# Linear attention with its output gate projected at another place, copies of turned tiles on ScalarE, and rows of scales made in two steps

## The chip, the cores and the metric

One core of a Trainium2 chip runs the whole program. The metric is the device time of one execution in microseconds (us), lower is better. Engines are named as in the profile: PE is TensorE, DVE is VectorE, ACT is ScalarE, POOL is GpSimd, SP issues most DMAs. PEld is PE's weight load, which runs beside its matmuls.

## What is computed

Four transformer-like layers over 256 tokens of 1024 numbers, all in float32: a forgetting attention and an MLP, a latent attention (MLA) and an MLP, then a gated linear attention (GLA) with a convolutional MLP and a short-convolution mixer with another one. The change touches GLA most:

```python
def gla_mixer(h, w_in, w_gate_up, b_gate, head_norm_g, w_out):
    proj = h @ w_in
    q, k, v, g, a_low = ...                 # widths 512, 512, 1024, 1024, 16
    log_a = jax.nn.log_sigmoid(a_low @ w_gate_up + b_gate) / 16.0
    bcum = jnp.cumsum(lc, axis=3)           # inside chunks of 64 tokens
    q_in = qc * jnp.exp(bcum)
    k_in = kc * jnp.exp(-bcum)
    scores = jnp.where(mask, jnp.einsum('bhncd,bhnsd->bhncs', q_in, k_in), 0.0)
    o_intra = jnp.einsum('bhncs,bhnse->bhnce', scores, vc)
    k_dec = kc * jnp.exp(b_last[..., None, :] - bcum)
    chunk_kv = jnp.einsum('bhncd,bhnce->bhnde', k_dec, vc)
    ...                                     # a scan over 4 chunks adds o_inter
    o = o * lax.rsqrt(jnp.mean(o * o, axis=-1, keepdims=True) + RMS_EPS)
    o = o * head_norm_g * jax.nn.silu(g)
    return o @ w_out
```

## The kernel before

**Matmuls in three parts.** Each weight tile is loaded raw by SP's queue, rounded to a high part on ACT (`wh`, L294) and subtracted to a low part on DVE (`wl`, L312). Each activation is split the same way (`hh` L509 or L1373, `hl` L512 or L1374). Each product is three matmuls: high by high, high by low, low by high (L339). A unit is two blocks of 128 weight rows; there are five buffers for split units, and `unit` casts four units ahead, at the call that takes a unit.

**Projections.** `proj` multiplies 8 blocks of activations by a weight block of 512 columns for two groups of 128 tokens (t = 0 and 1): after each t of each block, three matmuls, it calls `tick`, so a projection has 16 ticks. Its results stand in two of the three PSUM banks of the tag `up`; after the last block of each t an `evac` function reads them. `proj_T` makes the turned product (features in partitions) with 96 matmuls of 256 columns, 16 ticks as well; `proj_wide` one of 528 columns. `accum` is the output projection into four banks of the tag `acc`; of its inputs `y` it first takes blocks 0 to 3 and then 4 to 7.

**Deferred steps.** `after(n, f)` puts a step n ticks later into the order of the program. `force` runs the deferred steps at once where something that is asked for isn't emitted yet (`Act.get` does this for an operand). The tile framework then fixes each engine's order at compile time, by its own estimate of when each instruction is ready, with the order of the program as priority; on the chip each engine runs that order and waits where an operand is late.

**GLA before** (`gla`, L1151): `proj_wide` gives the first half of v and the 16 gate columns; `proj` of the second half of v follows, and beside it `gates` and `gates2` (two rounds of a log-sigmoid chain of DVE and ACT steps, a scaling by 1/16 at L1205, a scan at L1208, four exponentials). Then `proj_T` of k into acc banks and of q into up banks (`ev_k`, `ev_q` multiply by a row of scales, L416 and L419), then `proj` of the first half g0 of the output gate with the side program `core` beside it, and then `proj` of its second half g1. `core` makes one step per tick from tick 4 of the projection it stands beside: scores, states, at tick 12 the outputs `o` of heads 0 and 1 with their square sums, at tick 13 those of heads 2 and 3. `ev_g` applies Silu on ACT (L1248) and, some ticks later, the head gain on DVE (L1251); `fin` multiplies the outputs by their root scale and the gate (L1342); `prep` turns the result on PE into the one bank of tag `tp` (L523), and `split` makes `hh` on ACT and `hl` on DVE from that bank. Then `accum` runs.

**Rows of scales.** `make_row` (L137) copies two columns of scales wide on DVE (L144), turns them on PE with `transpose4` in the same step, and copies the row out on ACT (L148). There are seven in the program.

**Attention.** `pT` (L721) turns probabilities into two banks; DVE empties one (L725), ACT the other (L726). There are 12 calls. MLA also turns its rotated keys (L1035) and queries (L1072) and empties those banks on DVE.

Of the kernel before, what the change touches and what calls it, by code (L numbers as in the profile page):

```python
# [11 lines left out]
F32 = mybir.dt.float32  # L12
# [6 lines left out]
P = 128  # L19
# [100 lines left out]
class Cols:  # L120


    def __init__(self, kb, tile):
        self.kb, self.tile, self.ok, self.rows = kb, tile, set(), {}
# [12 lines left out]
    def make_row(self, c, tp=None):  # L137

        if c in self.rows:
            return  # L140
        kb, nc = self.kb, self.kb.nc
        self.wait(c, c + 2)
        wide = kb.tmp_tile()
        nc.vector.tensor_copy(wide[:, :S].rearrange("p (t n) -> p t n", t=2),  # L144
                              self.tile[:, c:c + 2].unsqueeze(2).to_broadcast([P, 2, P]))
        tp = kb.transpose4(wide, 2, tp if tp is None else lambda: tp)
        row = kb.small.tile([P, S], F32, tag="rowb", name=kb.name("rowb"), bufs=2)
        nc.scalar.copy(row, tp[:, :S])  # L148
        self.rows[c] = row

    def row(self, c, n=2):

        while c not in self.rows:
            if c in self.ok and c + 1 in self.ok:
                self.make_row(c)
            else:
                self.kb.force()
        return self.rows[c].unsqueeze(1).to_broadcast([P, n, S])


class Builder:
# [559 lines left out]
    def pT(self, p):  # L721
        pt = self.att.tile([P, 768], F32, tag="pT", name=self.name("pT"), bufs=2)
        tps = self.halves([p[:, i * P:(i + 1) * P] for i in range(6)], (self.tp_tile, self.attention_tile))
        out = pt.rearrange("p (b j c) -> p b j c", j=2, c=64)
        self.nc.vector.tensor_copy(out[:, :, 0], tps[0])  # L725
        self.nc.scalar.copy(out[:, :, 1], tps[1])  # L726
        return pt
# [265 lines left out]
    def mla(self, h, rs, hook):  # L993
# [21 lines left out]
        def ev_kv(t, ps):  # L1015
# [8 lines left out]
            def rot():  # L1024

                kr = self.tmp_tile(S)
                k3 = kr.rearrange("p (t c) -> p t c", t=2)
                self.rope(k3[:, :, 0:64], kc.rearrange("p (t c) -> p t c", t=2), None, 2)
                nc.vector.tensor_copy(k3[:, :, 64:128], k3[:, :, 0:64])

                def tr():
                    tp = turned()[:, 0:S]
                    for i in range(2):
                        nc.tensor.transpose(tp[:, i * P:(i + 1) * P], kr[:, i * P:(i + 1) * P], self.ident)
                    nc.vector.tensor_copy(krT, tp)  # L1035
                    self.marks.update((("kr", 0), ("kr", 1)))
                self.after(DLY[9], tr)
# [26 lines left out]
        def ev_rope(t, ps):  # L1064
# [5 lines left out]
            def tr():  # L1070
                tp = self.transpose4(o)
                nc.vector.tensor_copy(qr.rearrange("p (k s) -> p k s", k=4)[:, :, t * P:(t + 1) * P],  # L1072
                                      tp.rearrange("p (k s) -> p k s", k=4))
                self.marks.add(("qr", t))
# [68 lines left out]
    def plan_gla(self):  # L1143
        w = self.a["gla_w_in_2"][0]
        self.add_proj(self.a["gla_w_va"], 8, 0, WIDE)
        for c in (1536, 512, 0, 2048, 2560):
            self.add_proj(w, 8, c, 512)
        self.plan_rows(self.a["gla_w_out_2"][0], 0, 4)
        self.plan_rows(self.a["gla_w_out_2"][0], 4, 4)

    def gla(self, h, rs, hook):  # L1151
# [38 lines left out]
        def gates2():  # L1190
# [6 lines left out]
            for j in range(2):  # L1197
                zs = self.tmp_tile()
                for i in range(2):
                    nc.vector.tensor_scalar(out=zs[:, i * S:(i + 1) * S], in0=z[2 * j + i][:, 0:S],  # L1200
                                            scalar1=bg[:, 2 * j + i:2 * j + i + 1], scalar2=None, op0=ALU.add)
# [3 lines left out]
                nc.vector.tensor_scalar(out=o, in0=o, scalar1=1.0 / 16.0, scalar2=None, op0=ALU.mult)  # L1205
# [4 lines left out]
            nc.scalar.activation(out=E, in_=B, func=AF.Exp)  # L1210
            nc.scalar.activation(out=Ei, in_=B, func=AF.Exp, scale=-1.0)
            b4 = B.rearrange("p (n c) -> p n c", c=64)
            bl = b4[:, :, 63:64]
            nc.scalar.activation(out=dec, in_=bl.rearrange("p n c -> p (n c)"), func=AF.Exp)
            nc.vector.tensor_tensor(out=Ed.rearrange("p (n c) -> p n c", c=64), in0=bl.to_broadcast([P, 16, 64]),
                                    in1=b4, op=ALU.subtract)
            nc.scalar.activation(out=Ed, in_=Ed, func=AF.Exp)

        self.after(DLY[16], gates)
        self.proj(h, 8, 512, ev_v(1))  # L1220
# [22 lines left out]
        y = Act(self)  # L1243

        def ev_g(i):
            def f(t, ps):
                gs = self.tmp_tile()
                nc.scalar.activation(out=self.like(gs, ps), in_=ps, func=AF.Silu, scale=rs[:, t:t + 1])  # L1248

                def gain():  # L1250
                    nc.vector.tensor_tensor(out=gs, in0=gs, in1=hg[:, i * 512:(i + 1) * 512], op=ALU.mult)  # L1251
                    self.after(DLY[20], lambda: fin(t, i, gs))

                self.after(DLY[19], gain)
            return f

        oo = {}
# [3 lines left out]
        def core():  # L1261
# [56 lines left out]
            for j in range(2):  # L1318
# [15 lines left out]
                self.rsqrt(hr[:, 4 * j:4 * j + 4], hs[:, 4 * j:4 * j + 4])  # L1334
                yield 1

        def fin(t, j, gs):
            o = oo.pop((t, j))
# [12 lines left out]
        self.proj(h, 8, 512, ev_g(0))  # L1351
        while self.side is not None:
            self.step()
        self.proj(h, 8, 512, ev_g(1))
# [398 lines left out]
```

## Time and profile before

| what | us |
|---|---|
| median of 3 runs (lowest to highest) | 1104.21 (1104.09 to 1104.54) |
| the profiled execution | 1104.49 |
| its span, first to last instruction | 1102.7 |
| mean granted TensorE clock | 0.997 |
| PE busy in the span | 1087.3 |
| DVE busy | 801.4 |
| ACT busy | 609.2 |

1.8 us of the profiled execution lie outside its span. Matmuls are pipelined, and the profile models their ends: a row's duration is longer than the distance to the next start, so PE's lost time is read from start to start, and a wait row shows a little less than was lost.

### The profile page before, as it was taken

To read this page: it belongs to the slowest core of one execution; us is meant where nothing else is said; L and a number is where in the kernel's file an instruction comes from. 1 tells how busy PE (TensorE), PEld (TensorE's weight loads), DVE (VectorE), ACT (ScalarE), POOL (GpSimd) and SP (SyncE) were. 2 spreads that over 40 slices of the span, in tenths; PEclk is the share of its full clock that TensorE was granted. 3 is DMA by queue.
4 is the path that set the end of the run, shared out by engine and by line. 5 is a ranking of instruction groups with operands and counts; after the bars stand their busy time and mean duration, and the time that the engine had idled before them with its cause. 6 is when DMAs were issued, how large, how long until landed. Compare 5 with 4: busy or idle time off the path is not lost.

```text
span 1102.7 us, 19201 instructions
## 1 busy us (share of the span) xinstructions
PE 1087.3 (99%) x7769; PEld 1003.4 (91%) x7769; DVE 801.4 (73%) x1200; ACT 609.2 (55%) x927; POOL 30.4 (3%) x55
## 2 busy tenths in 40 slices
PE   9999999999999999999999999999999999999997
PEld 7987999999988999999897899999999999999996
DVE  6687756556687766555788578787787768987786
ACT  6466655445665555545664556555555446565563
POOL 1000000000000000000010000000000000000001
PEclk9999999999999999999999999999999999999998
DMA  9844466655563566665555354566665664657551
GB/s 335 298 165 145 162 195 206 210 193 173 142 207 128 172 192 204 206 200 192 194 180 183 108 178 155 179 197 217 201 220 193 197 204 153 189 194 224 188 166 74
DMA packets 137801, 207.30 MB, mean 188 GB/s; under 512 B 10528, under 2 KB 65008, under 8 KB 137712
## 3 DMA queue, kind: packets, MB, share of 16 engines
q1 hardware_dynamic: 136576, 203.89, 56.8%
q10 hardware_dynamic: 1136, 2.17, 0.5%
q8 instruction: 61, 1.00, 0.4%
q14 instruction: 28, 0.23, 0.1%
HBM read 204.97 MB, written 1.07 MB: 187 GB/s over the span
## 4 chain that ended last, share of the span: by engine, by line
PE 87%; DVE 7%; ACT 2%; DMA 1%; issue 1%; SPq 0%; ACTq 0%; DVEq 0%
PE up L339 52%; PE acc L339 33%; DVE wl L312 2%; DMA raw<-fox_w_in 1%; ACT wh L294 1%; PE acc L523 1%; PE tp L523 1%; ACT p L697 1%; DVE p L716 1%; DVE x L602 0%; DVE p L707 0%; PE tp L533 0%; DVE tmp L1365 0%; DVE pT L725 0%; DVE kT L1232 0%
## 5 line engine op out<-in xcount | busy, mean ns | idle before, releaser
L312 DVE TENSOR_TENSOR wl<-raw,wh 128x1024 fp32r<-128x1024 f32 (+2 forms) x373 | 452.3, 1219 | 223.4 <-ACT wh L294 222.4
L294 ACT CAST wh<-raw 128x1024 fp32r<-128x1024 f32 (+2 forms) x373 | 388.8, 1043 | 381.7 <-PE up L339 253.1
L339 PE MATMUL up<-hh,wh 128*128 128x256 f32 x1564 | 431.7, 276 | 0.0
L339 PE MATMUL up<-hh,wl 128*128 128x256 f32 x1564 | 430.1, 275 | 0.0
L339 PE MATMUL up<-hl,wh 128*128 128x256 f32 x1564 | 429.4, 275 | 0.0
L339 PEld LDWEIGHTS up<-hh,wh 128*128 128x128 f32 x1564 | 300.1, 192 | 2.9 <-issue 1.5
L339 PEld LDWEIGHTS up<-hh,wl 128*128 128x128 f32 x1564 | 300.1, 192 | 0.9
L339 PEld LDWEIGHTS up<-hl,wh 128*128 128x128 f32 x1564 | 299.8, 192 | 0.3 <-DVE hl L512 0.2
L339 PE MATMUL acc<-wh,hh 128*128 128x512 f32 (+1 forms) x606 | 227.4, 375 | 0.2 <-DVE mx L716 0.2
L339 PE MATMUL acc<-wh,hl 128*128 128x512 f32 (+1 forms) x606 | 225.1, 371 | 0.1
L339 PE MATMUL acc<-wl,hh 128*128 128x512 f32 (+1 forms) x606 | 224.8, 371 | 0.0
L339 PEld LDWEIGHTS acc<-wh,hl 128*128 128x128 f32 x606 | 114.5, 189 | 15.4 <-DVE hl L1374 0.5
L339 PEld LDWEIGHTS acc<-wh,hh 128*128 128x128 f32 x606 | 114.6, 189 | 15.0 <-DVE mx L716 0.6
L339 PEld LDWEIGHTS acc<-wl,hh 128*128 128x128 f32 x606 | 114.7, 189 | 13.4
L1365 DVE SCALAR_TENSOR_TENSOR tmp<-tmp,vecs,tmp 128x255 f32<-128x255 f32 x192 | 78.0, 479 | 15.2 <-ACT tmp L1363 15.2
L339 PE MATMUL up<-wh,hh 128*128 128x512 f32 (+4 forms) x142 | 52.2, 370 | 1.8 <-DVE tmp L419 1.8
L339 PE MATMUL up<-wl,hh 128*128 128x512 f32 (+4 forms) x142 | 49.9, 352 | 0.2 <-DVE wl L312 0.2
L339 PE MATMUL up<-wh,hl 128*128 128x512 f32 (+4 forms) x142 | 49.8, 353 | 0.1
L1363 ACT ACTIVATE tmp<-tmp,vecs 128x256 f32<-128x256 f32 x96 | 40.9, 496 | 0.0
L1373 ACT CAST hh<-tmp 128x512 fp32r<-128x512 f32 x58 | 34.1, 619 | 8.3 <-DVE tmp L1418 8.3
L1374 DVE TENSOR_TENSOR hl<-tmp,hh 128x512 fp32r<-128x512 f32 x58 | 38.3, 685 | 0.0
L339 PEld LDWEIGHTS up<-wh,hh 128*128 128x128 f32 x142 | 26.8, 189 | 8.1 <-issue 5.5
(205 smaller groups left out, 769.8 us busy)
## 6 DMA issues: line engine op xcount, KB each, us to landing
raw<-ffn_w_up SPq DMA_DIRECT2D x176, 256.0 KB, 4.2
raw<-ffn_w_up SPq DMA_DIRECT2D x32, 1024.0 KB, 5.3
raw<-ffn_w_down SPq DMA_DIRECT2D x32, 1024.0 KB, 5.0
raw<-ffn_w_down SPq DMA_DIRECT2D x44, 512.0 KB, 6.6
raw<-sc_w_in SPq DMA_DIRECT2D x12, 1024.0 KB, 5.3
raw<-fox_w_in SPq DMA_DIRECT2D x10, 1024.0 KB, 9.7
raw<-gla_w_in SPq DMA_DIRECT2D x10, 1024.0 KB, 5.0
raw<-fox_w_out SPq DMA_DIRECT2D x4, 1024.0 KB, 5.2
```

Source lines behind the costliest of these rows:

```text
L294: self.last_hi = nc.scalar.copy(hi[:, :kn, :w], self.raws[r][:, k:k + kn])
L312: self.last_wl = nc.vector.tensor_tensor(out=u.lo[:, :kn, :w], in0=self.raws[r][:, k:k + kn], in1=u.hi[:, :kn, :w].bitcast(F32), op=ALU.su ...
L339: self.nc.tensor.matmul(out, lhsT, rhs, start=start, stop=stop, skip_group_check=True)
L523: self.nc.tensor.transpose(tp[:, i * P:(i + 1) * P], src[:, i * P:(i + 1) * P], self.ident)
L697: self.nc.scalar.activation(out=p[:, o:o + n], in_=p[:, o:o + n], func=AF.Exp, scale=scale, bias=nm[:, j:j + 1], accum_out=sm[:, j:j + 1])
L716: self.nc.vector.tensor_tensor_reduce(out=p[:, o:o + n], in0=lgs[h][:, w], in1=bias(h)[:, w], scale=1.0, scalar=NEG, op0=ALU.add, op1=ALU. ...
L1363: nc.scalar.activation(out=out, in_=z, func=AF.Copy, scale=w[:, 2:3])
L1365: nc.vector.scalar_tensor_tensor(out=out[:, d:], in0=z[:, :S - d], scalar=w[:, 2 - d:3 - d], in1=out[:, d:], op0=ALU.mult, op1=ALU.add)
L1373: nc.scalar.copy(hi, src)
L1374: nc.vector.tensor_tensor(out=lo, in0=src, in1=hi.bitcast(F32), op=ALU.subtract)
```

## The change

1. In GLA the weight block of g0 (column 2048) is planned and projected ahead of the second half of v; g1 is now the projection beside `core`, and nothing stands between it and the output projection. The gate g0 is kept in the two buffers of tag `pT` until `fin`; `fin(t, 0)` is deferred by 4 + t ticks from the step that makes the outputs of heads 0 and 1, and no longer by the gate. 
2. In `gates2` the bias is added on ACT (Identity), and the scaling by 1/16 is folded into the exponentials.
3. `make_row` defers its transpose and copy by 3 ticks behind the wide copy.
4. `pT` empties both banks on ACT; MLA's turned keys and queries are emptied on ACT.

```diff
-    def make_row(self, c, tp=None):
-
-        if c in self.rows:
+    def make_row(self, c, tp=None, gap=3):
+
+        if c in self.asked:
             return
+        self.asked.add(c)
...
-        tp = kb.transpose4(wide, 2, tp if tp is None else lambda: tp)
-        row = kb.small.tile([P, S], F32, tag="rowb", name=kb.name("rowb"), bufs=2)
-        nc.scalar.copy(row, tp[:, :S])
-        self.rows[c] = row
+
+        def turn():
+            bank = kb.transpose4(wide, 2, None if tp is None else lambda: tp)
+            row = kb.small.tile([P, S], F32, tag="rowb", name=kb.name("rowb"), bufs=2)
+            nc.scalar.copy(row, bank[:, :S])
+            self.rows[c] = row
+
+        kb.after(gap, turn)
...
-        self.nc.vector.tensor_copy(out[:, :, 0], tps[0])
-        self.nc.scalar.copy(out[:, :, 1], tps[1])
+        for j, tp in enumerate(tps):
+            self.nc.scalar.copy(out[:, :, j], tp)
...
-                    nc.vector.tensor_copy(krT, tp)
+                    nc.scalar.copy(krT, tp)
...
-                nc.vector.tensor_copy(qr.rearrange("p (k s) -> p k s", k=4)[:, :, t * P:(t + 1) * P],
-                                      tp.rearrange("p (k s) -> p k s", k=4))
+                nc.scalar.copy(qr.rearrange("p (k s) -> p k s", k=4)[:, :, t * P:(t + 1) * P],
+                               tp.rearrange("p (k s) -> p k s", k=4))
...
-        for c in (1536, 512, 0, 2048, 2560):
+        for c in (2048, 1536, 512, 0, 2560):
...
-                    nc.vector.tensor_scalar(out=zs[:, i * S:(i + 1) * S], in0=z[2 * j + i][:, 0:S],
-                                            scalar1=bg[:, 2 * j + i:2 * j + i + 1], scalar2=None, op0=ALU.add)
+                    nc.scalar.activation(out=zs[:, i * S:(i + 1) * S], in_=z[2 * j + i][:, 0:S], func=AF.Identity,
+                                         bias=bg[:, 2 * j + i:2 * j + i + 1])
...
-                nc.vector.tensor_scalar(out=o, in0=o, scalar1=1.0 / 16.0, scalar2=None, op0=ALU.mult)
...
-            nc.scalar.activation(out=E, in_=B, func=AF.Exp)
-            nc.scalar.activation(out=Ei, in_=B, func=AF.Exp, scale=-1.0)
+            nc.scalar.activation(out=E, in_=B, func=AF.Exp, scale=1.0 / 16.0)
+            nc.scalar.activation(out=Ei, in_=B, func=AF.Exp, scale=-1.0 / 16.0)
...
+        def ev_g(i):
+            def f(t, ps):
+
+                gs = self.tmp_tile() if i else self.att.tile([P, 768], F32, tag="pT", name=self.name("gs"), bufs=2)[:, :512]
+                nc.scalar.activation(out=self.like(gs, ps), in_=ps, func=AF.Silu, scale=rs[:, t:t + 1])
+
+                def gain():
+                    nc.vector.tensor_tensor(out=gs, in0=gs, in1=hg[:, i * 512:(i + 1) * 512], op=ALU.mult)
+                    gates_of[t, i] = gs
+                    if i:
+                        self.after(DLY[20], lambda: fin(t, i))
+
+                self.after(DLY[19], gain)
+            return f
+
+        self.proj(h, 8, 512, ev_g(0))
         self.proj(h, 8, 512, ev_v(1))
...
+                if j == 0:
+                    for t in range(2):
+                        self.after(4 + t, lambda t=t: fin(t, 0))
                 yield 1
...
         self.side = core()
-        self.proj(h, 8, 512, ev_g(0))
+        self.proj(h, 8, 512, ev_g(1))
         while self.side is not None:
             self.step()
-        self.proj(h, 8, 512, ev_g(1))
         acc = self.new_acc()
```

## Rows read from the trace of the kernel before

**Rows 1.** The page: its busy times by engine, and the chain's shares.

```profile
PE 1087.3 (99%) x7769; PEld 1003.4 (91%) x7769; DVE 801.4 (73%) x1200; ACT 609.2 (55%) x927; POOL 30.4 (3%) x55
...
PE 87%; DVE 7%; ACT 2%; DMA 1%; issue 1%; SPq 0%; ACTq 0%; DVEq 0%
```

**Rows 2.** Chain of waits in order of time: start us, us, what.

```profile
142.62 10.36 PE acc L339 x48
```

**Rows 3.** Waits of PE: line, what it waited for, us, times, longest us.

```profile
PE up L339 <- DVE tmp L419: 1.8, 1, 1.8
...
PE tp L533 <- DVE pT L725: 0.6, 1, 0.6
PE up L339 <- DVE pT L725: 0.5, 1, 0.5
PE tp L523 <- DVE tmp L144: 0.4, 1, 0.4
```

**Rows 4.** Timeline of PE from q to g0: start us, us, line, instruction.

```profile
590.80 0.38 PE L339 MATMUL up<-wh,hl 128*128 128x512 f32 x1
592.93 0.45 PE L339 MATMUL up<-wh,hh 128*128 128x512 f32 x1 [1.75 <-DVE tmp L419]
```

**Rows 5.** Timeline of DVE, the same stretch.

```profile
589.76 2.36 DVE L312 TENSOR_TENSOR wl<-raw,wh 128x1024 fp32r<-128x1024 f32 x2
592.03 1.08 DVE L419 SCALAR_TENSOR_TENSOR tmp<-up,rowb 128x256 f32<-128x256 f32 x3
```

**Rows 6.** Windows over k and q: length, PE, PEld, DVE, ACT, POOL, clock, DMA, GB/s.

```profile
568.60:580.00 11.40, 11.40 (x103) 11.35 (x102) 11.37 (x19) 7.31 (x11) 0.00 (x0) 1.00 0.49 151
580.00:591.00 11.00, 11.00 (x98) 10.75 (x96) 11.00 (x16) 7.21 (x9) 0.00 (x0) 1.00 0.45 152
```

**Rows 7.** Timeline of PE: end of g0, first transposes of y.

```profile
617.98 0.38 PE L339 MATMUL up<-wh,hl 128*128 128x512 f32 x1
...
622.72 0.60 PE L523 MATMUL tp<-ident,tmp 128*128 128x128 f32 x4
```

**Rows 8.** Timeline of ACT around that end.

```profile
617.38 1.28 ACT L1248 ACT_TABLE_LOAD   x1
618.68 0.69 ACT L1248 ACTIVATE tmp<-up,rs 128x512 f32<-128x512 f32 x1
619.26 0.38 ACT L556 ACTIVATE junk<-acc 128x256 f32<-128x256 f32 x1
...
619.62 0.69 ACT L1248 ACTIVATE tmp<-up,rs 128x512 f32<-128x512 f32 x1
620.19 2.06 ACT L294 CAST wh<-raw 128x1024 fp32r<-128x1024 f32 x2
623.36 0.58 ACT L509 CAST hh<-tp 128x512 fp32r<-128x512 f32 x1 [1.12 <-PE tp L523]
```

**Rows 9.** Timeline of POOL and DVE, the same stretch and the next.

```profile
620.23 1.01 POOL L563 TENSOR_TENSOR hr<-hr,mhalf 128x4 f32<-128x4 f32 x1
...
624.67 0.69 DVE L512 TENSOR_TENSOR hl<-tp,hh 128x512 fp32r<-128x512 f32 x1
...
630.96 1.65 DVE L1342 SCALAR_TENSOR_TENSOR tmp<-acc,hr,tmp 128x256 f32<-128x256 f32 x4
```

**Rows 10.** Timeline of ACT, evacuation of the second half of v.

```profile
568.74 1.25 ACT L616 ACTIVATE v<-up,rs 128x512 f32<-128x512 f32 x2
```

**Rows 11.** Single lines: count, duration ns min/median/max, first and last start.

```profile
L725 DVE COPY pT<-tp x12: 546/549/553, 63.1 to 361.4; 128x384 f32<-128x384 f32 x12
...
L726 ACT COPY pT<-acc x8: 459/472/478, 63.1 to 339.7; 128x384 f32<-128x384 f32 x8
...
L1200 DVE TENSOR_SCALAR tmp<-acc,vecs x4: 476/480/484, 563.1 to 571.0; 128x256 f32<-128x256 f32 x4
```

**Rows 12.** Timeline of ACT and DVE: a row of scales and its first reader.

```profile
659.94 0.37 ACT L148 COPY rowb<-tp 128x256 f32<-128x256 f32 x1
...
664.11 1.28 DVE L416 TENSOR_TENSOR tmp<-up,rowb 128x512 f32<-128x512 f32 x2
```

More of the change, by code (lines that the diff above doesn't have):

```diff
@@ L123, in __init__ @@
     def __init__(self, kb, tile):
-        self.kb, self.tile, self.ok, self.rows = kb, tile, set(), {}
+        self.kb, self.tile, self.ok, self.rows, self.asked = kb, tile, set(), {}, set()
     def set(self, *cols):
@@ L145, in make_row @@
                               self.tile[:, c:c + 2].unsqueeze(2).to_broadcast([P, 2, P]))
-        tp = kb.transpose4(wide, 2, tp if tp is None else lambda: tp)
-        row = kb.small.tile([P, S], F32, tag="rowb", name=kb.name("rowb"), bufs=2)
-        nc.scalar.copy(row, tp[:, :S])
-        self.rows[c] = row
+        def turn():
[4 more added lines that the diff above has]
+        kb.after(gap, turn)
     def row(self, c, n=2):
         while c not in self.rows:
-            if c in self.ok and c + 1 in self.ok:
+            if c in self.ok and c + 1 in self.ok and c not in self.asked:
                 self.make_row(c)
@@ L1209, in gates2 @@
                                                  op0=ALU.mult, op1=ALU.add)
-            nc.scalar.activation(out=E, in_=B, func=AF.Exp)
-            nc.scalar.activation(out=Ei, in_=B, func=AF.Exp, scale=-1.0)
+            nc.scalar.activation(out=E, in_=B, func=AF.Exp, scale=1.0 / 16.0)
+            nc.scalar.activation(out=Ei, in_=B, func=AF.Exp, scale=-1.0 / 16.0)
             b4 = B.rearrange("p (n c) -> p n c", c=64)
             bl = b4[:, :, 63:64]
-            nc.scalar.activation(out=dec, in_=bl.rearrange("p n c -> p (n c)"), func=AF.Exp)
+            nc.scalar.activation(out=dec, in_=bl.rearrange("p n c -> p (n c)"), func=AF.Exp, scale=1.0 / 16.0)
             nc.vector.tensor_tensor(out=Ed.rearrange("p (n c) -> p n c", c=64), in0=bl.to_broadcast([P, 16, 64]),
                                     in1=b4, op=ALU.subtract)
-            nc.scalar.activation(out=Ed, in_=Ed, func=AF.Exp)
+            nc.scalar.activation(out=Ed, in_=Ed, func=AF.Exp, scale=1.0 / 16.0)
         self.after(DLY[16], gates)
+        y = Act(self)
+        oo, gates_of = {}, {}
+        def ev_g(i):
[10 more added lines that the diff above has]
+        self.proj(h, 8, 512, ev_g(0))
         self.proj(h, 8, 512, ev_v(1))
@@ L1241, in ev_q @@
             self.after(DLY[18], f)
[L1243 to L1257, printed above, removed]
         hs = self.small.tile([P, 8], F32, tag="hs", name="hs", bufs=1)
@@ L1334, in core, with fin @@
                 self.rsqrt(hr[:, 4 * j:4 * j + 4], hs[:, 4 * j:4 * j + 4])
+                if j == 0:
+                    for t in range(2):
+                        self.after(4 + t, lambda t=t: fin(t, 0))
                 yield 1
-        def fin(t, j, gs):
-            o = oo.pop((t, j))
+        def fin(t, j):
+            o, gs = oo.pop((t, j)), gates_of.pop((t, j))
             yy = self.tmp_tile()
```

## The prediction

> **What bounds the kernel now.** I read the page first: PE is busy for 99% of the span and DVE for 73%, and 87% of the chain that ended last is PE [rows 1]. So the time moves only where PE is made to wait, and an engine's saved work is worth nothing by itself. The chain of waits gives PE's full pace: 48 matmuls of 512 columns in 10.36 us, 0.216 us each [rows 2], while a row calls one busy for 0.38 us [rows 4]; a wait row behind such a matmul thus shows about 0.16 us less than was lost. The third view is PE's own waits [rows 3]: five of them end in instructions that this change moves or removes, and these are the whole stock from which it can gain. The timeline then shows each wait's cause, and the windows whether the engine behind it is full.
>
> **The wait between q and g0 (gain 1.9).** g0's first three matmuls go into the free `up` bank, the next three need the bank that q's first half still holds. From the start at 590.80 to the next at 592.93 are 2.13 us, less the pace of 0.216: 1.91 us are lost [rows 4]. The bank is emptied by L419, which is ready when q ends but stands behind two low-part subtractions, until 592.03 [rows 5]. DVE has no gap there: it is busy 11.37 of 11.40 us and 11.00 of 11.00 us over k and q [rows 6], because the chain of `gates2` runs on into k and q. With g0 ahead of the second half of v the chain gets 48 more matmuls, 10.36 us, before k ends [rows 2], and loses two scalings and four additions of 0.48 us [rows 11]. Then L419 stands behind at most one subtraction, and no such wait is due. I take the whole 1.9; the bounds are 0 (DVE just as late, whatever stands there) and 1.9.
>
> **Waits for DVE in turned tiles (gain 2.5).** Two waits of 0.6 and 0.5 us end in L725, two of 0.4 in L144, of which one row stands [rows 3]; with 0.16 for each modelled end they are 1.9 + 0.6 = 2.5 us. For L725 the bank waits because DVE has subtractions ahead of the copy; ACT empties the second bank sooner each time. ACT takes 0.472 us for the same shape that takes DVE 0.549 [rows 11], so 12 copies put 5.7 us on an engine that is busy for 55% of the span [rows 1]. (The Trainium skill, ScalarE: Activation LUTs, Rules for kernel authors, says to use VectorE rather than ScalarE for simple arithmetic; for these float32 copies out of PSUM the row says the contrary.) An exponential that is queued behind a second copy comes 0.47 us later; its reader, the next turn of the probabilities, is some four ticks off. For L144 the two-step row puts 3 ticks, 9 matmuls or 1.9 us at the pace of [rows 2], between the wide copy and the transpose, more than either wait. The price is a later row: in the convolutional MLP it is copied at 659.94 and first read at 664.11 [rows 12], so 2 us more still fit, and one cast of 1 us as well. MLA's three other copies go the same way, end in no wait of PE's list and are taken at nothing: matmuls of the next projection hide them, and without that cover each costs at most its own length, by the copy of a bank on ACT 0.58 [rows 8]. I take 2.5; bounds: 0 (the time comes back at the next step of the same attention chain) and 2.5, and a loss of 1 if exponentials are pushed behind copies on a path that has no slack, two copies of 0.47.
>
> **The price: nothing between g1 and the output projection (loss 3.2).** Before, 48 matmuls of g1 lie between `core` and the first use of `y`. After, the first output matmul needs `hh` of y's first four blocks: transposes, copy on ACT. Those transposes stand behind all of g1 in the order of the program, since `fin(0, 0)` comes at its last tick and `prep` five ticks on. Put the end of the projection beside `core` where it is in this trace, 617.98 + 0.22 = 618.20 [rows 7]. PE's four transposes take 0.44 us (0.60 [rows 7] less the modelled end of 0.16), to 618.64, and their result can be read from 618.84 (622.72 to 623.36 are 0.64 [rows 7, 8]). ACT then still has the table load that Silu needs, two Silus with a square sum between them, to 620.19 [rows 8], and, ahead of the copy by the order of the program, one weight cast (`accum` takes its unit before it asks for `y`), 2.06/2 = 1.03 us [rows 8]: to 621.22. The copy itself takes 0.58 [rows 8]: to 621.80. PE has nothing else, so it is idle from 618.64 to about 621.85: **3.2 us**. After that it has 16 matmuls of token group 0 that need only `hh` (3.5 us at the pace), and `hl` and the other group should come beside them. Bounds: 0.8, if the copy runs as soon as its bank can be read (0.64 + 0.58 - 0.44), and 7.4, worked out at the slower rival.
>
> **Table loads (no cost in the sum).** Silu of g0 now stands between the two rounds of the log-sigmoid chain, whose Exp and Ln use another table; the trace has one load of 1.28 us in GLA [rows 8], and there would be three: 2.6 us more on ACT. ACT is idle 4.1 of 11.4 and 3.8 of 11.0 us there [rows 6], and casts are four units ahead, some 10 us of PE's work, so the load hides; if the cover fails it is the third rival.
>
> **The rest, no cost each.** The raw loads in SP's queue change order (one block of g0 ahead of v) but not number or size. The buffers of tag `pT` are long free, the gain row is fetched at GLA's start, and the four Identity steps on ACT replace DVE steps of 0.48 us [rows 11] while nothing waits for either.
>
> **Sum.** -1.9 - 2.5 + 3.2 = -1.2 us on the profiled execution of 1104.49: 1103.3. The median of the runs is 0.28 below that execution, so I forecast 1103.0 for the median. A measurement of this kernel can tell about 0.2%, 2.2 us, from no change: this is inside.
>
> **Rivals.**
> *The tail is covered (faster).* If the framework's order lets the `hh` copy pass the cast, or runs it between the Silus, the idle time is 0.8 to 2.2 us instead of 3.2. For it: ACT's order before shows a square sum between two Silus, so steps do slip in. Against: in the order of the program the cast is first. With 1.0: -1.9 - 2.5 + 1.0 = -3.4, 1100.8.
> *The tail runs in series (slower).* One bank serves all four turns of `y`. The second token group's transposes wait until `hl` of the first has read it, and on DVE that `hl` can stand behind the second halves' `fin`: its root scale is ready at 620.23 + 1.01 = 621.24, the four multiplications take 1.65 [rows 9], one subtraction 1.2, so `hl` runs 624.1 to 624.7 where it started 1.3 after `hh` here (623.36 to 624.67 [rows 8, 9]); transposes and copy of the second group, 1.2 more, end at 626.0. If the fixed order makes PE wait for both, the loss is 626.0 - 618.64 = 7.4 us, and -4.4 + 7.4 = +3.0: 1107.2. For it: the wait at 591 shows that the order is kept when DVE runs late. Against: 12 to 16 matmuls of the first group can go between. It decides the sign from 4.4 us of tail on, and is slower by over 0.2% from 6.6.
> *The loads are on the path.* The evacuation at 568.74 [rows 10] comes a load later, 1.28 us, the second token group of the next projection waits for that bank, and 1.3 us are lost: -1.2 + 1.3, 1104.3. The Trainium skill (ScalarE: Activation LUTs, Table sets) speaks against this change here: it says to finish with one set of functions before switching, and under What ACT_TABLE_LOAD costs it puts a switch at about 2.66 us with a drain; by that figure the result would be an estimated 1105.7. In this trace Silu starts 0.02 us behind the end of a load of 1.28 us [rows 8], so no drain shows there, and the row decides.
> *Nothing is gained at q.* If DVE is as late as before at the end of q, the 1.9 stays: 1104.9.
>
> **How the numbers follow.** Forecast 0.40 (1101.8 to 1104.3); covered tail 0.30; series 0.17; loads 0.08; nothing at q 0.05. Faster by over 0.2% (below 1102.0): the covered tail and a little of the forecast, 0.33. Slower (above 1106.4): most of the series case and a mishap of two small ones, 0.17. Within: 0.50. The range leaves out a tenth at either side: down to 1099.5 (tail 0.8, and some relief for DVE beyond the named waits), up to 1107.0.
>
> **What would show it.** Right: no wait of PE for L419, L725 or L144 in its list of waits; PE idle between the last matmul of g1 and the first `acc` matmul of about 3 us, ended by ACT `hh` L509; three table loads in GLA. Wrong: an idle PE behind g0's Silu, a wait for `hl` on DVE in the tail, or PE waits in attention on ACT's copies. The prediction fails most easily by the tail's size, which the order fixed at compile time decides.

## The result, and the profile after

| | before | after |
|---|---|---|
| median, us (lowest to highest; runs) | 1104.38 (1104.09 to 1104.57; 4) | 1114.22 (1113.46 to 1116.01; 4) |
| the profiled execution, us | 1104.49 | 1113.46 |
| its span, us | 1102.7 | 1111.6 |

The ratio is 1.0092 (95% interval 1.0080 to 1.0104): the change makes the kernel 0.9% slower. The forecast was 1103.0, with a range up to 1107.0. The line numbers of the changed kernel stand 5 to 12 above those of before in the lines named here: L339 is L344, L523 is L528, L509 and L512 are L514 and L517, L704, L707 and L716 are L709, L712 and L721, L1342 is L1354, L616 (ACT's copies of scaled results out of PSUM) is L621. `ev_g` moved up: its Silu and gain, L1248 and L1251 before, are L1232 and L1235.

The page after, busy times by engine:

```profile
PE 1091.7 (98%) x7769; PEld 1006.3 (91%) x7769; DVE 793.0 (71%) x1179; ACT 620.9 (56%) x950; POOL 30.3 (3%) x55
```

Against [rows 1] DVE has 8.4 us less work, ACT 11.7 more, and PE, with the same 7769 instructions, is busy for 4.4 us longer in a span that is 8.9 longer. So PE waits longer and also runs slower somewhere. Its waits (line, what it waited for, us, times, longest us), the answer to [rows 3]:

```profile
PE acc L344 <- DVE mx L721: 2.7, 1, 2.7
PE tp L528 <- DVE tmp L1354: 2.2, 1, 2.2
PE tp L528 <- DVE hl L517: 1.4, 1, 1.4
...
PE acc L344 <- ACT hh L514: 0.7, 1, 0.7
...
PE up L344 <- ACT gs L1232: 0.4, 1, 0.4
```

The five waits of [rows 3] that I wanted gone are gone. In their place stand a wait in the forgetting attention (the first row), three in GLA's tail, and a small one behind the Silu of g0. To place the loss I set the two traces side by side at fixed steps of the program, such as a layer's last addition to x. The changed kernel stands 1.4 us behind when the first projection starts, 2.8 at the end of the forgetting attention, 2.5 at the start of GLA, 9.2 at its end and 9.0 at the end of the program. So the attention costs 1.4 and GLA 6.8. Inside GLA, 1.85 us are won up to the end of g1, about what was forecast for q, and 8.6 are lost behind it. The 1.4 at the start are not of the edits: up to there the engines of both kernels run the same instructions, and the first one that the change touches (a row's wide copy) runs at 22.25 us. What differs is the run: the granted clock is full from 9.54 us on there and from 4.26 in the trace of before.

The profiled execution of the changed kernel is the fastest of its four and shows the highest mean clock of them (0.996 against 0.991 to 0.994). So the trace accounts for 9.0 us, where the medians differ by 9.8.

**The tail.** Timeline of PE after (start us, us, line, instruction, [idle before, releaser]):

```profile
629.84 0.38 PE L344 MATMUL up<-wh,hl 128*128 128x512 f32 x1
632.41 0.83 PE L528 MATMUL tp<-ident,tmp 128*128 128x128 f32 x4 [2.19 <-DVE tmp L1354]
633.91 0.57 PE L344 MATMUL acc<-wh,hh 128*128 128x512 f32 x1 [0.68 <-ACT hh L514]
634.28 0.63 PE L344 MATMUL acc<-wl,hh 128*128 128x512 f32 x1
636.35 1.11 PE L528 MATMUL tp<-ident,tmp 128*128 128x128 f32 x4 [1.44 <-DVE hl L517]
```

From start to start, less the pace, the three gaps are 2.35, 0.89 and 1.85 us. The two engines behind them, ACT and then DVE:

```profile
629.25 1.28 ACT L1232 ACT_TABLE_LOAD   x1
630.54 0.69 ACT L1232 ACTIVATE tmp<-up,rs 128x512 f32<-128x512 f32 x1
```

```profile
631.26 0.69 DVE L1235 TENSOR_TENSOR tmp<-tmp,row 128x512 f32<-128x512 f32 x1 [8.89 <-ACT tmp L1232]
631.87 1.65 DVE L1354 SCALAR_TENSOR_TENSOR tmp<-acc,hr,gs 128x256 f32<-128x256 f32 x4
633.44 0.68 DVE L1235 TENSOR_TENSOR tmp<-tmp,row 128x512 f32<-128x512 f32 x1
634.04 1.66 DVE L1354 SCALAR_TENSOR_TENSOR tmp<-acc,hr,tmp 128x256 f32<-128x256 f32 x4
635.61 0.68 DVE L517 TENSOR_TENSOR hl<-tp,hh 128x512 fp32r<-128x512 f32 x1
```

DVE does nothing for 8.89 us, and then first multiplies g1's gate by the head gain (L1235), which needs the Silu of g1, which needs the table load. Only then come the multiplications of heads 0 and 1 (`gs`, L1354), although their root scale was there at 626.61:

```profile
625.60 1.01 POOL L568 TENSOR_TENSOR hr<-hr,mhalf 128x4 f32<-128x4 f32 x1
```

They need nothing of g1: in an experiment below, where they stand earlier in the order, they start at 623.85, right when that root scale is there (622.80 + 1.01). The order fixed at compile time put them behind. Then `hl`, which holds the only `tp` bank, stands behind the four multiplications of heads 2 and 3. DVE took nothing out of order here: for 4.65 of its 8.89 idle us, from 626.61 on, the multiplications could have run. The Trainium skill (TensorE: Matmul & The Clock Gate, Architectural detail: the array is 16× 32×32, not 1× 128×128) says that DVE's queue is strictly first in, first out. The row with 8.89 us agrees.

And the clock. Windows after (length, then PE, PEld, DVE, ACT and POOL busy, granted clock, DMA share, GB/s):

```profile
628.00:630.00 2.00, 2.00 (x10) 1.62 (x9) 0.00 (x0) 1.92 (x7) 0.00 (x0) 1.00 0.06 22
630.00:632.00 2.00, 0.22 (x2) 0.00 (x0) 0.74 (x2) 1.99 (x5) 0.32 (x1) 1.00 0.00 0
...
634.00:636.00 2.00, 0.91 (x2) 0.21 (x2) 2.00 (x6) 0.00 (x0) 0.00 (x0) 0.54 0.00 0
636.00:638.00 2.00, 1.65 (x6) 1.56 (x7) 1.43 (x2) 0.50 (x1) 0.00 (x0) 0.50 0.04 8
638.00:640.00 2.00, 2.00 (x6) 1.54 (x6) 0.69 (x1) 0.09 (x1) 0.00 (x0) 0.50 0.00 0
```

After PE was nearly idle from 630 to 632, the granted clock falls from 2.4 to 1.2 GHz at 634.17, for 6.83 us, and the 2 us from 638 hold 6 instructions where those from 628 held 10. My sum had no such term. 4.65 us of the 6.83 lie behind 636.35, the start of the second turn (the transposes of y for the second token group). From there on PE waits no more, and at half the pace these 4.65 us cost an estimated 2.3.

**The forgetting attention.** PE, then DVE, after:

```profile
93.30 0.38 PE L344 MATMUL acc<-wh,hl 128*128 128x512 f32 x1
96.42 0.48 PE L344 MATMUL acc<-wh,hh 128*128 128x512 f32 x1 [2.75 <-DVE mx L721]
```

```profile
94.59 0.18 DVE L709 RECIPROCAL rc<-sm 128x4 f32<-128x4 f32 x1 [1.99 <-ACT p L702]
94.81 1.01 DVE L712 TENSOR_SCALAR p<-p,rc 128x128 f32<-128x128 f32 x4
95.73 0.28 DVE L721 CUSTOM_DVE_ANT_0 p<-acc,bias 128x128 f32<-128x128 f32 x1
```

The masking L721 must empty the `acc` banks of the scores before PE can go on. It now stands behind the reciprocal and the normalization of another head, which wait 1.99 us for exponentials. In the kernel before, masking stood ahead of both, behind the copy L725:

```profile
92.93 0.28 DVE L716 CUSTOM_DVE_ANT_0 p<-acc,bias 128x128 f32<-128x128 f32 x1
...
94.54 0.18 DVE L704 RECIPROCAL rc<-sm 128x4 f32<-128x4 f32 x1 [0.42 <-ACT p L697]
```

### The profile page after: what moved, and what is told of

Read it like the earlier page. It is cut to its first block, busy times and chain, and to the rows that moved or that the text cites. A ratio compares the mean times of both kernels' runs of the same rounds, so it can differ in the third digit from the quotient of the medians.

```text
span 1111.6 us, 19202 instructions
## 1 busy us (share of the span) xinstructions
PE 1091.7 (98%) x7769; PEld 1006.3 (91%) x7769; DVE 793.0 (71%) x1179; ACT 620.9 (56%) x950; POOL 30.3 (3%) x55
## 4 chain that ended last, share of the span: by engine, by line
PE 86%; DVE 7%; ACT 3%; DMA 2%; issue 1%; POOL 0%; SPq 0%; ACTq 0%; DVEq 0%
PE up L344 50%; PE acc L344 34%; DVE wl L317 2%; PE acc L528 1%; DMA bias<-rows 1%; ACT p L702 1%; ACT wh L299 1%; DVE p L721 1%; DVE p L712 1%; PE tp L528 1%; DMA raw<-mla_w_q_b 0%; DVE x L607 0%; ACT junk L561 0%; DMA x<-x 0%; DVE tmp L1376 0%
## 5 line engine op out<-in xcount | busy, mean ns | idle before, releaser
L344 PE MATMUL up<-hh,wh 128*128 128x256 f32 x1564 | 432.0, 276 | 0.4 <-DVE kT L421 0.4
L344 PE MATMUL up<-hl,wh 128*128 128x256 f32 x1564 | 430.1, 276 | 0.5 <-DVE hl L517 0.5
L344 PE MATMUL up<-hh,wl 128*128 128x256 f32 x1564 | 430.5, 275 | 0.0
L344 PEld LDWEIGHTS up<-hh,wh 128*128 128x128 f32 x1564 | 300.3, 192 | 3.4 <-issue 1.5
L344 PEld LDWEIGHTS up<-hh,wl 128*128 128x128 f32 x1564 | 300.3, 192 | 0.9
L344 PEld LDWEIGHTS up<-hl,wh 128*128 128x128 f32 x1564 | 300.0, 192 | 1.0 <-DVE hl L517 0.9
L344 PE MATMUL acc<-wh,hh 128*128 128x512 f32 (+1 forms) x606 | 228.5, 377 | 3.4 <-DVE mx L721 2.7
L344 PE MATMUL acc<-wh,hl 128*128 128x512 f32 (+1 forms) x606 | 225.8, 373 | 0.2
L344 PE MATMUL acc<-wl,hh 128*128 128x512 f32 (+1 forms) x606 | 225.8, 373 | 0.0
L344 PEld LDWEIGHTS acc<-wh,hh 128*128 128x128 f32 x606 | 115.2, 190 | 18.4 <-DVE mx L721 3.1
L344 PEld LDWEIGHTS acc<-wh,hl 128*128 128x128 f32 x606 | 115.0, 190 | 15.9 <-DVE hl L1385 0.5
L344 PEld LDWEIGHTS acc<-wl,hh 128*128 128x128 f32 x606 | 115.1, 190 | 13.4
L344 PE MATMUL up<-wh,hh 128*128 128x512 f32 (+4 forms) x142 | 52.5, 371 | 0.6 <-ACT gs L1232 0.4
L344 PE MATMUL up<-wl,hh 128*128 128x512 f32 (+4 forms) x142 | 49.8, 350 | 0.2 <-DVE wl L317 0.2
L344 PE MATMUL up<-wh,hl 128*128 128x512 f32 (+4 forms) x142 | 49.7, 353 | 0.1
L344 PEld LDWEIGHTS up<-wh,hh 128*128 128x128 f32 x142 | 26.9, 189 | 7.2 <-issue 3.3
```

Of the source, the lines that this page charges most:

```text
L344: self.nc.tensor.matmul(out, lhsT, rhs, start=start, stop=stop, skip_group_check=True)
```

## The experiments

Line numbers are each kernel's own. Each kernel is compared with runs of the kernel before on the same chip (median 1104.1 to 1104.3). "GLA stretch" is the time in a trace from the start of the second token group's copy of the gate columns on DVE to the start of GLA's last addition to x: 93.1 us before, 99.8 after.

### Which part costs

Four kernels: before with one part of the change each. The first has all edits in `gla` and its plan (parts 1 and 2), the second only `pT`, the third only `make_row`, the fourth only MLA's turned keys and queries.

> The kernel before with the changes inside gla alone (g0 ahead of the second half of v, bias and scaling off DVE, fin of the first heads deferred from core). Theory: the tail behind g1 carries the loss by itself: GLA's end, read at the last x add of its output projection, moves by +8.7 - 1.9 = +6.8 us and the kernel takes 1111.2; PE's start behind g1 waits for fin on DVE and the granted clock falls to half behind it. Rival: the tail is slow only together with the rows in two steps or the moved copies: 1104 to 1106.

> The kernel before with both halves of the turned probabilities copied on ACT, nothing else. Theory: DVE's fixed order in the forgetting attention now has the normalisation ahead of the last masking, which holds an acc bank: PE waits about 2.9 us for DVE L716 near 92 us, the attention's end moves by +1.8 us, MLA by -0.3: 1105.7. Rival, the prediction's own step: the two waits on L725 go and nothing comes instead: 1103.0. Second rival: the rows in two steps made the new order, this one shows neither: 1104.2.

> The kernel before with make_row's transpose and copy three ticks behind its wide copy, nothing else. Theory: three waits on L144 go and nothing else changes: -1.0 us, 1103.3. Rival: the later turns change the fixed order in the forgetting attention and bring the 2.9 us wait there: 1106.

> The kernel before with MLA's turned keys and queries copied on ACT, nothing else. Theory: no wait of PE ends in them, so within 0.3 us of before: 1104.3. Rival: they free a full DVE ahead of the first logits: 1103.5 or less. In all four: the granted clock in the first 10 us is that of before (full from about 4 us); if it rises only near 9.5 us in some of them, the 1.4 us that the changed kernel loses at the start are not of its edits.

| part alone | median, us | against before | ratio, 95% interval |
|---|---|---|---|
| GLA | 1111.10 | +6.9 | 1.0045 to 1.0075 |
| `pT` | 1106.57 | +2.4 | 1.0011 to 1.0030 |
| rows of scales | 1104.90 | +0.7 | 0.9998 to 1.0017 |
| MLA's keys and queries | 1103.80 | -0.4 | 0.9985 to 1.0004 |

The sum is +9.5, the whole change +9.8: the parts add up. Two of them carry the loss, and their traces show the tail and the masking wait as above. The rows came out 1.6 us above what I expected of them and MLA's copies 0.5 below, and neither fits its theory or its rival; both intervals include 1. The ten runs of the `pT` kernel fall into five of 1105.3 to 1106.1 and five of 1107.1 to 1107.5. The one that was profiled (1107.13) has the clock halved for 3.4 us from 94.96 on, at the end of the masking wait; no run of the lower five was profiled, so that the fall makes the difference is likely (the mean clocks, 0.997 to 0.999 in the lower five and 0.996 to 0.997 in the upper, fit) and not shown.

### What makes the tail

**The place in DVE's order.** The GLA part alone, with the multiplications of heads 0 and 1 three ticks sooner in the order of the program, and their turn two ticks behind them and no longer five:

```diff
-                        self.after(4 + t, lambda t=t: fin(t, 0))
+                        self.after(1 + t, lambda t=t: fin(t, 0))
...
-            self.after(DLY[21], lambda: self.prep(yy, t, list(range(4 * j, 4 * j + 4)), [(y, None)]))
+            self.after(DLY[21] if j else 2, lambda: self.prep(yy, t, list(range(4 * j, 4 * j + 4)), [(y, None)]))
```

> The GLA part alone (it ran at 1111.1 us), with the four multiplications of heads 0 and 1 put three ticks sooner into the order of the program and their turn 2 ticks behind them, not 5. Nothing else. The profile showed their operands ready some 5 us before they ran, with the gain of the second gate half (which waits for a table load and a Silu) ahead of them in DVE's fixed order. Theory (the loss in the tail is made by that order): they run beside the last matmuls of g1, the first turn of y is done when g1 ends, the wait of 2.2 us and the one of 0.7 behind it go, TensorE stays at its higher clock, and the kernel lands at 1102.5 to 1105.5. Rival (the tail is a series by its nature: cast, copy, one bank for all four turns): at most 1 to 2 us come back, 1108.5 to 1111.

Measured: 1107.13 us (1106.14 to 1109.33), ratio 1.0026 (1.0017 to 1.0036). 4.0 of the 6.9 us come back; it is above the upper end of what the theory gave, by 1.6. In the profiled execution (1106.47) the first turn of y runs beside the last matmuls of g1, and the clock stays at full:

```profile
626.60 0.60 PE L523 MATMUL tp<-ident,tmp 128*128 128x128 f32 x4
...
627.47 0.38 PE L339 MATMUL up<-wh,hl 128*128 128x512 f32 x1
629.32 0.48 PE L339 MATMUL acc<-wh,hh 128*128 128x512 f32 x1 [1.47 <-ACT hh L509]
```

```profile
628.00:630.00 2.00, 0.68 (x2) 0.30 (x2) 0.69 (x1) 2.00 (x6) 1.04 (x2) 1.00 0.00 0
630.00:632.00 2.00, 0.55 (x6) 0.54 (x6) 1.67 (x4) 0.79 (x1) 0.30 (x1) 1.00 0.00 0
```

The order was the largest cause. But the wait for `hh` is now 1.5 (its copy stands behind the load and a Silu on ACT), and that for `hl` 1.4: the next two links are late. I had expected the wait of 0.7 for `hh` to go, and it grew. The ten runs fall into two groups, five of 1106.1 to 1106.5 with a mean clock of 0.998 and five of 1107.8 to 1109.3 with 0.994 to 0.997. So the clock probably fell in the second five; only one of the first five was profiled.

**The table load.** The GLA part alone with Relu in place of Silu for g1's gate. It leaves out that Silu and its load:

```diff
-                nc.scalar.activation(out=self.like(gs, ps), in_=ps, func=AF.Silu, scale=rs[:, t:t + 1])
+                nc.scalar.activation(out=self.like(gs, ps), in_=ps, func=AF.Relu if i else AF.Silu, scale=rs[:, t:t + 1])
```

> The GLA part alone (1111.1 us), with Relu in place of Silu for the second gate half: it leaves out that Silu, and with it the table load of 1.28 us at the end of g1; the orders of the engines stay. Theory (the load is one link of the chain load, Silu, gain, multiplications, turn): the turn comes 1.3 us sooner, the wait of 2.2 us falls to about 0.9, and 1.3 to 4 us come back, the more so if TensorE's clock then doesn't fall: 1107 to 1110. Rival (the load is hidden beside the last matmuls of g1, and something else is late): 1110.5 to 1111.5.

Measured: 1109.33 us, 1.8 less than the GLA part. The wait for the multiplications falls from 2.2 to 1.3 us, where I expected 0.9; the one for `hl` grows from 0.9 to 1.6, and the clock falls all the same. The GLA stretch is 98.5 us in both traces. Yet the load was on the path. Counted from the start of the stretch (559.86 and 559.09), the second turn starts after 73.96 us in the GLA part and after 73.02 with Relu, 0.94 sooner (first the GLA part, then Relu):

```profile
633.82 1.12 PE L523 MATMUL tp<-ident,tmp 128*128 128x128 f32 x4 [0.93 <-DVE hl L512]
```

```profile
632.11 1.12 PE L523 MATMUL tp<-ident,tmp 128*128 128x128 f32 x4 [1.60 <-DVE hl L512]
```

What took the 0.94 back is the clock. It is at half for 6.83 us in both traces, but with Relu it falls later in the stretch: 4.83 of these us lie behind the start of the second turn, against 2.92. At half the pace that is 0.95 us more. The two profiled executions differ by 0.8, and that much the one with Relu is ahead before GLA begins. The profiled execution of the GLA part lies 1.0 below its median, the one with Relu at its own; why the medians differ by 1.8 stays open beyond that.

**Idle time or clock.** The GLA part alone with 14 spare matmuls in a free bank behind g1, 13 of them ahead of the end of y's first turn:

```diff
+        def spare(n):
+            for _ in range(n):
+                self.mm(idle[0], self.last_h[0], self.last_u.hi[:, 1, :512], True, True)
+
+        def turn(yy, t, j):
+            if not j:
+                idle[:] = idle or [self.up_tile()]
+                spare((9, 3)[t])
+            self.prep(yy, t, list(range(4 * j, 4 * j + 4)), [(y, None)])
+            if not j and not t:
+                spare(2)
```

> The GLA part alone (1111.1 us), with 14 spare matmuls of 512 columns (3.0 us at full pace) put into a free bank behind g1, 13 of them ahead of the first turn of y, where TensorE waited 2.2 and 0.7 us. Nobody reads their result. Theory (a good part of the loss isn't the idle time itself but the halved clock for 6.8 us after it, some 3.4 us): the spare matmuls fill the wait, the granted clock stays at full, and although there is 3.0 us more work the kernel gets faster, to 1107 to 1109. Rival (the matmuls behind the wait are slow because their operands come late, and the granted clock only mirrors that): 1110.8 to 1113.

Measured: 1108.58 us, 2.5 less than without the 3.0 us of spare work. The granted clock stays at full throughout, although PE then still waits 0.4 and 1.3 us:

```profile
626.69 2.97 PE L339 MATMUL up<-wh,hh 128*128 128x512 f32 x12
...
631.01 0.48 PE L339 MATMUL acc<-wh,hh 128*128 128x512 f32 x1 [0.44 <-ACT hh L510]
```

The GLA stretch falls from 98.5 to 97.2. In both traces the second turn starts 73.96 us into the stretch, so what is gained comes behind it, where PE waits no more and only its pace differs. So a part of the loss is the clock and not the idle time: 1.3 us by the two traces, 2.5 by the medians. The rival (a mirror of late operands) would have made the kernel slower.

**Closing the tail.** The GLA part with the earlier multiplications, y turned in banks of `up`, a Silu of one column behind the last exponential (so the load comes at 589.45, beside matmuls), and MLA's copies on ACT:

```diff
-            self.after(DLY[21], lambda: self.prep(yy, t, list(range(4 * j, 4 * j + 4)), [(y, None)]))
+            self.after(DLY[21] if j else 2, lambda: self.prep(yy, t, list(range(4 * j, 4 * j + 4)), [(y, None)], self.up_tile))
...
             nc.scalar.activation(out=Ed, in_=Ed, func=AF.Exp, scale=1.0 / 16.0)
+            hot = self.small.tile([P, 1], F32, tag="hot", name="hot", bufs=1)
+            nc.scalar.activation(out=hot, in_=Ed[:, 1023:1024], func=AF.Silu)
```

> The GLA part with the four multiplications of heads 0 and 1 sooner (as in the run at 1107.1 us), and two more edits in the tail: y is turned in banks of the tag up and no longer in the one bank of tp, and a Silu of one column right behind the last exponential takes the table load out of the tail. Beside it MLA's copies on ACT, as in the run above; the forgetting attention and the rows stay as before. Theory (the 1.6 us behind ACT's hh are the load with its Silu, the 1.6 us behind DVE's hl are the one bank): both waits fall below 0.6 us, the tail costs at most 1, and with the 1.9 us won at q the kernel lands at 1102 to 1104. Rival (with those gone the next link, the weight cast or the second halves' multiplications, is late by as much): 1104.5 to 1106.5.

Measured: 1105.02 us, ratio 1.0008 (0.9999 to 1.0018). The rival was nearer. PE's waits in GLA:

```profile
PE up L523 <- DVE tmp L1351: 0.9, 1, 0.9
PE up L339 <- DVE tmp L419: 0.6, 1, 0.6
PE up L339 <- DVE hl L512: 0.2, 1, 0.2
```

The tail is down to 1.4 us from start to start; the rest is the multiplications of the second heads, the rival's own example. And the wait at q, L419, is back with 0.6: there DVE runs four subtractions in a row ahead of it. The stretch is 94.0 us, 0.9 above before. Even so mended, the moved g0 costs: the next section has the kernel with part 2 and MLA's copies, but with the old order of the projections, at 1102.20, 2.8 us less.

### What the wait at q hung on

Before with part 2 alone (bias on ACT, scaling folded into the exponentials), and then that with MLA's copies, `pT`'s included, on ACT; `pT` in MLA had been run by itself as well:

```diff
-        self.nc.vector.tensor_copy(out[:, :, 0], tps[0])
+        (self.nc.scalar.copy if ("kr", 0) in self.marks else self.nc.vector.tensor_copy)(out[:, :, 0], tps[0])
```

> The kernel before, with the first of the two banks of turned probabilities emptied on ACT in MLA alone; the forgetting attention keeps DVE and ACT. With ACT in both attentions the kernel ran at 1106.6 against 1104.2, and the profile had a new wait of 2.9 us in the forgetting attention for the last masking on DVE. Theory (that one wait is the whole loss, and in MLA the copy on ACT gains its 0.6 us): 1103.4 to 1104.2, no wait for L725 in MLA. Rival (the copies on ACT cost wherever they stand): 1104.6 to 1106.

> The kernel before with the second part of the change alone: the bias added on ACT, the scaling by 1/16 folded into the exponentials; the order of the projections is that of before. It asks whether the wait of 1.9 us between q and g0 goes because g0 stands ahead of the chain of gate steps, or because that chain is shorter (two scalings and four additions of 0.48 us less on DVE, of 2.9 us in all). Theory A (the moved g0 is what frees DVE at the end of q): the wait stays at 1 to 2 us, 1103.5 to 1104.5. Theory B (2.9 us less work on DVE is enough): the wait goes, 1102.0 to 1103.0.

> The kernel before with the second part of the change, and in MLA alone the copies on ACT (turned keys, queries, both banks of probabilities). By theory B on the wait between q and g0 and by what MLA's parts gave alone (0.3 to 0.5 us each): 1101.2 to 1103.0, the fastest kernel yet. By theory A: 1103.0 to 1104.2. If the small gains in MLA were only the spread of the runs: 0.8 more in either case.

`pT` on ACT in MLA alone: 1103.90, ratio 0.9995 (0.9986 to 1.0005), not to be told from no change. Part 2 alone: 1102.66, ratio 0.9986 (0.9977 to 0.9995), 1.6 us faster. Both together: 1102.20 (ratio 0.9974 to 0.9992). In the trace of part 2 alone only this is left of the 1.8 of [rows 3]:

```profile
PE up L339 <- DVE tmp L419: 0.3, 1, 0.3
```

```profile
591.19 0.38 PE L339 MATMUL up<-wh,hl 128*128 128x512 f32 x1
591.86 0.45 PE L339 MATMUL up<-wh,hh 128*128 128x512 f32 x1 [0.30 <-DVE tmp L419]
```

From start to start the loss at q falls from 1.91 to 0.46 with the projections in their old order. 2.9 us less work on DVE are enough (theory B); moving g0 can add at most the 0.46 that is left. And since the GLA part is part 2 with the moved g0, the move by itself costs 8.4 us (1111.10 against 1102.66).

### One copy in the forgetting attention

Before, with both banks of `pT` on ACT in the forgetting attention but for the fifth of its six calls:

```diff
-        self.nc.vector.tensor_copy(out[:, :, 0], tps[0])
+        self.calls = getattr(self, 'calls', 0) + 1
+        (self.nc.vector.tensor_copy if self.calls == 5 or self.calls > 6 else self.nc.scalar.copy)(out[:, :, 0], tps[0])
```

> The kernel before with both banks of turned probabilities emptied on ACT in the forgetting attention, but for one call, the fifth of its six, which keeps DVE; MLA as before. That one copy gives DVE's fixed order back its place of the masking ahead of the reciprocal and the four multiplications there. Theory (the new wait of 2.9 us, and the halved clock that follows it in some runs, are made by that order alone): no such wait, 1103.9 to 1104.9 us. Rival (five of six copies on ACT make the attention late anyway): the wait is there or turns up elsewhere, 1105.3 to 1107.

Measured: 1103.48 us, ratio 0.9992 (0.9982 to 1.0002), against 1106.57 with all calls on ACT. DVE's order there, the answer to the rows of the changed kernel above:

```profile
92.38 0.28 DVE L716 CUSTOM_DVE_ANT_0 p<-acc,bias 128x128 f32<-128x128 f32 x1
...
94.45 0.18 DVE L704 RECIPROCAL rc<-sm 128x4 f32<-128x4 f32 x1 [0.88 <-ACT p L697]
```

The masking stands ahead of the reciprocal again, and the wait of 2.7 us is not in PE's list. Five of six copies on ACT cost nothing. This kernel also keeps DVE's copies in MLA, but those on ACT cost nothing by themselves (1103.90), and in the fastest kernel below, where the fifth call alone keeps DVE, the wait is missing as well. So the `pT` part lost its 2.4 us by where a single copy of 0.55 us put its neighbours in an order fixed beforehand, and by no engine being too busy.

### All that gains, with and without the rows

> The kernel before with the second part of the change, MLA's copies on ACT, and both banks of turned probabilities on ACT in all calls but the fifth of the forgetting attention. If the gains of the single pieces add up (second part 1.6 us, one DVE copy kept 0.8, MLA 0.4): 1101.0 to 1102.2. If the gain in the forgetting attention was only the spread of the runs: 1102.2 to 1102.8.

> The kernel above with the rows of scales in two steps as well. That is the changed kernel but for its first part (the order of the projections in GLA) and but for one copy of turned probabilities. Theory (these two alone make the changed kernel slower, the rows give and take about the same): 0 to 0.8 above the kernel above, 1101.0 to 1103.0. Rival (the rows in two steps cost where other copies are on ACT as well, which their run alone could not show): over 1103.0.

Measured: 1100.88 (1100.50 to 1101.22; ratio 0.9971, 0.9959 to 0.9982) without the rows in two steps and 1101.64 (1101.05 to 1102.16; ratio 0.9977, 0.9968 to 0.9986) with them. The first is just below what I expected of it, and beats both kernels, by 3.2 and 13.3 us. The second is the changed kernel but for its first part and one copy, so these two alone stand between 1114.2 and 1101.6. The rows cost 0.8 here, much as by themselves (0.7, not clear of the spread of the runs). With them:

```profile
21.74 0.66 PE L528 MATMUL tp<-ident,tmp 128*128 128x128 f32 x4 [0.99 <-ACT tmp L621]
```

Without them no wait for L621 is among PE's; two for L144 of 0.4 and 0.3 are. So the two waits of L144 do go, and PE waits for ACT instead, at the place of one of them. Whether that wait is all of the 0.8 is not shown.

## Why the prediction was wrong, point by point

**The wait between q and g0: right in size, half wrong in its reason.** -1.85 measured up to the end of g1, -1.9 forecast. I put the shorter chain beside the moved g0 as a second help. It was the main one: 1.45 of the 1.9 come with part 2 alone. Nor does the reader of the bank (L424) stand behind at most one subtraction: four run ahead of it, from 598.82 on, and it still starts at 603.90, before q's last matmul at 604.05. That the number came out so well is partly luck.

**The tail: the step that failed.** I set the first transposes of y right behind g1 ("to 618.64"), with ACT as the only thing late, and came to 3.2. The multiplications ahead of those transposes had no row in the sum, since `fin` was asked for in time. But in DVE's fixed order the gain of g1's gate, and with it Silu and table load, stood first: 2.35 us ahead of the transposes, where I had none. Behind them the weight cast that I priced at 1.03 hardly counted: `hh` started 0.16 us after its transposes could be read. Then `hl` stood behind the second heads' multiplications, which is the slower rival's mechanism: another 1.85. That rival had a chance of 0.17 and was the nearest of all, with 7.4 us against the 8.6 that were lost; it saw the one bank and the late `hl`, but not the first gap or the clock. Beside the three gaps (2.35, 0.89 and 1.85) 3.5 us are left: the lower clock, an estimated 2.3 behind the last gap, and smaller gaps. Two of the prediction's own signs of being wrong came true, an idle PE behind g0's Silu and a wait for `hl` in the tail. The run with the spare matmuls prices the clock at 1.3 to 2.5 us. The Trainium skill (TensorE: Matmul & The Clock Gate, Why this matters for your kernels) warns of long idle gaps between bursts of matmuls, since they bring the slow clock back. The traces agree in kind, but in the tail the clock fell around gaps of at most 2.35 us, shorter than those the skill warns of.

**The turned probabilities: wrong sign.** I forecast -1.4 for L725 and bounded the loss at 1, for exponentials pushed behind copies. The waits did go (0.8 from start to start in the forgetting attention), but the new one is 2.9. My list of who waits for a copy held its readers; it did not hold the instructions whose places in DVE's order hang on it.

**The rows of scales: no gain.** -1.1 forecast, +0.7 (not clear of the spread) and +0.8 measured: the row's 1.9 us of delay cover the wide copy, and the transpose then meets another wait, for ACT.

**Table loads.** Five in GLA, not three: one for the Silu of g0, then three for Exp, Ln and Exp of the second round of the log-sigmoid chain, and one for the Silu of g1. The first four cost little (0.4 for PE behind `gs`, which is what the third rival named, at a third of its price); the fifth stands in the tail. The Trainium skill (ScalarE: Activation LUTs, Table sets) asks to finish one set before switching. The runs show less than that: moving the fifth load beside matmuls was one of the edits that shortened the tail, and no run with the moved g0 took the other four away.

**The range.** It ended at 1107.0 because each case held one mishap. Here two were independent (GLA 6.9, `pT` 2.4), and each was a wait in the order of DVE.

## What to carry to other kernels

A step that is asked for in time need not run in time: look in the trace for what stands just ahead of it on its engine, and ask whether that waits for something new. Before moving work away from in front of the last dependent chain, count the whole chain behind it, with the bank that holds it, and add the slower matmuls that follow a gap. And take a change apart: the part that looked smallest (two scalings and four additions) held 1.45 of the 1.85 us won up to the end of g1, and half of what the fastest kernel gains.

## What the hardware showed

- The granted clock fell to 1.2 GHz for 6.83 us in the tail of three traces: in the GLA part at 629.91, right behind a gap of 2.35 us, in the run with Relu behind two gaps of 1.4 and 0.9, in the changed kernel behind two of 2.35 and 0.9. It did not fall around two gaps of 1.6 us in the trace with the earlier multiplications (the mean clocks of that kernel's slower runs suggest that there it did), nor where spare matmuls filled the first gap. One gap of 2.9 us in the forgetting attention brought 3.4 us at half clock in the trace of `pT` alone, and none in that of the changed kernel. So the length of a gap alone does not decide it in these traces.
- The start of the program varies: over the sixteen traces the clock is full from 4.3 to 9.5 us on, and the first projection's matmul starts between 10.8 and 12.9 us, ahead of any instruction that these kernels have changed. These 2.1 us are about 0.2% of this kernel, so one profile can't tell a change of that size; a step in the middle of the trace, beside the same step of another trace, can.
- In the kernel before, one table served Exp, Ln and Exp in both rounds. With a Silu between the rounds the second round takes a load for each of the three, 1.28 us each:

```profile
575.17 1.28 ACT L911 ACT_TABLE_LOAD   x1
...
579.00 1.28 ACT L915 ACT_TABLE_LOAD   x1
...
581.88 1.28 ACT L916 ACT_TABLE_LOAD   x1
```

- ACT empties a bank of 384 columns in 0.47 us where DVE takes 0.55 [rows 11]; with one copy left on DVE that exchange gained 0.8 us in the forgetting attention (the interval reaches from -0.2% to no change), with none left, in both attentions, it lost 2.4.
